# A hybrid decoder block: pacing copies on another engine, and level multiplications joined over two token halves

## The chip, the cores and the metric

The kernel runs on one core of a Trainium2 chip. TensorE (PE) multiplies matrices into PSUM, and its weight loads (PEld) overlap its multiplications. VectorE (DVE), ScalarE (ACT) and GpSimd (POOL) work on tiles in SBUF and PSUM, and SyncE (SP) issues most of the DMA transfers. Each engine runs its own list of instructions in the order in which it stands, and waits on semaphores for the other engines and for the DMAs. The metric is the time of one execution in microseconds (us).

## What is computed

One decoder layer on 256 tokens of width 1024, in float32. From one input projection two token mixers are fed, a gated linear recurrence (HGRN2) and an attention over blocks; both are projected, mixed through sigmoid gates, and followed by a layer norm, a SwiGLU network of width 2816 and a second layer norm. The parts that matter here:

```python
def hgrn2_mixer(q, f_logit, inp, lb):
    ...
    k = (1.0 - lb) * jax.nn.sigmoid(-z)
    qf = jax.nn.silu(q.astype(jnp.float32))
    ...
    def step(state, xs):
        qc, kc, vc, lfc = xs
        G = jnp.cumsum(lfc, axis=2)
        diff = G[:, :, :, None, :] - G[:, :, None, :, :]
        decay = jnp.exp(jnp.where(causal, diff, -jnp.inf))
        scores = jnp.einsum('bhtsd,bhtd,bhsd->bhts', decay, qc, kc)
        ...

def hybrid_layer(x, w_in, lb, ...):
    proj = jnp.einsum('bsd,dn->bsn', x, w_in)
    hq, hf, hi, hg, mq, mk, mv, gate_logits = jnp.split(proj, offsets, axis=-1)
    o_a = hgrn2_mixer(...)
    y_a = rms_norm(o_a, ...) * jax.nn.silu(hg)
    ...
    mixed = jnp.einsum('bsc,cd->bsd', g_a * z_a + g_b * z_b, w_out)
    x = layer_norm(DN_ALPHA * x + mixed, ln1_w, ln1_b)
    ...
    return layer_norm(DN_ALPHA * x + y, ln2_w, ln2_b)
```

## The kernel before

**The weight stream.** All weights are cut into 89 blocks of 1 MB (128 x 2048 floats), used in a fixed order. `stage` brings one in: SyncE loads it into one of three raw buffers (line 233), ScalarE casts it to a rounded high half `wh` (line 236), and VectorE subtracts that from the raw block for the low half `wl` (line 238). There are four buffers for each half. A product with such a weight is made of three matmuls, high by high, high by low and low by high. When the subtraction of a block ends, its raw buffer is free, and the load of the block three places on can be issued. Blocks are counted from 0 below.

**The weight sums.** Three of the big projections (hg, mv and the last one of the feed-forward network) are done in seven block products where eight would be usual (`quad_stage`, `quad_product`). They need sums of weight blocks, which GpSimd makes with 32 DMA transfers into DRAM, some of them copies and some with addition. `sum_weights` (line 247) issues one of them, paced by the weight stream. A tick, one element of a staged block, is copied into `ticks` (line 253); GpSimd adds it to itself into `mark` (line 254), and only then issues the transfer (line 256). `SUMS_WITH` names the block for each tick; most are blocks 2 to 16 and 56 to 67.

**The recurrence.** `hgrn_steps` (line 478) works out the scores in seven levels. On level l the tokens are taken in groups of n = 2^l. `KL` gathers the keys of the earlier groups (line 506, ScalarE), TensorE multiplies them with the queries of the later ones (line 514), VectorE writes the results into `SD` under a mask (line 516), and then the queries `Qt` and the keys `Kt` are multiplied by the groups' totals of the forget gate (lines 524 and 525, VectorE). The totals for the next level are products of pairs (line 528). The tokens are in two halves of 128, the second of them in reverse order, so the offsets in the two halves differ, and the multiplications of lines 524 and 525 run once for each half. Each step of the recurrence is woven between two stages of the weight stream.

**The stage of hg and ga.** Blocks 12 to 22 alternate between products for hg (`quad_stage`, line 607) and pairs of the gate ga (`gate_pair`, line 642). Block 17 is the fourth product of hg: lines 623 and 624 take it out of PSUM on VectorE. Block 18 is the fifth; line 627 stands behind block 18's product in the text, but needs only results up to block 17. Block 19 is for ga, block 20 for hg, block 21 for ga and block 22 for hg. The silu of hg (line 665, ScalarE) comes when a part of it is complete.

**What sets the order.** Outside of a few stretches that are written out by hand, a scheduler orders the instructions of each engine by its own estimate of times. So a change in one place can move instructions that it does not name.

Of the kernel before, what the change touches and what calls it, by code (L numbers as in the profile page):

```python
# [17 lines left out]
P = 128  # L18
T = 256
NT = T // P  # L20
D = 1024
KC = D // P
H = 8
# [121 lines left out]
def hybrid_layer_kernel(ctx: ExitStack, tc, x, xw, vecs, wts, ln1_w, ln1_b, ln2_w, ln2_b, consts, out):  # L145
    nc = tc.nc
# [16 lines left out]
    def r32(ap):  # L163
        return ap.bitcast(F32)
# [52 lines left out]
    def stage(pieces=None, eng=nc.vector):  # L217
        i = state["next"]
        if i >= len(loads):
            return  # L220
        state["next"] += 1
        at, k, held = loads[i]
        src = source(at).rearrange("p (k c) -> p k c", k=k)
        view = lambda z: z.rearrange("p (k c) -> p k c", k=k)
        home, tag = (late, "late") if state.get("four") and i % 4 == 0 else (wraw, "raw")
        raw = view(home.tile([P, 2048], F32, tag=tag, name=f"raw{i}"))
        if held:
            h, l = view(slot(f"wh{i}", F32R)), view(slot(f"wl{i}", F32R))
        else:
            h = view(whi.tile([P, 2048], F32R, tag="h", name=f"wh{i}"))  # L230
            l = view(wlo.tile([P, 2048], F32R, tag="l", name=f"wl{i}"))
        for ks in ks_of(pieces or (k,)):
            load = nc.sync.dma_start(raw[:, ks, :], src[:, ks, :])
            if i < EARLY:
                tc.keep_in_program_order(load)
            nc.scalar.copy(h[:, ks, :], raw[:, ks, :])  # L236
            yield
            eng.tensor_sub(l[:, ks, :], raw[:, ks, :], r32(h[:, ks, :]))  # L238
            yield
        ready.append((h, l))  # L240
        for _ in range(SUMS_WITH.count(i)):
            sum_weights(r32(l[:, 0, 0:1]))

    mark = cp.tile([P, 1], F32, tag="mark", name="mark")
    ticks = cp.tile([P, len(sums)], F32, tag="ticks", name="ticks")
# [1 line left out]
    def sum_weights(behind):  # L247


        n = len(SUMS_WITH) - len(sums)  # L250
        dst, src, add = sums.pop(0)
        tick = ticks[:, n:n + 1]
        nc.vector.tensor_copy(tick, behind)  # L253
        tc.keep_in_program_order(nc.gpsimd.tensor_tensor(mark, tick, tick, op=ALU.add))  # L254
        more = dict(accum_op=ALU.add, max_dma_last_dim=2048) if add else {}
        tc.keep_in_program_order(nc.gpsimd.dma_start(source(dst), source(src), **more))  # L256
# [151 lines left out]
    Fg, Kt, Qg = halves(slot("Fg")), halves(slot("Kt")), halves(slot("Qg"))  # L408
# [28 lines left out]
    for j in range(4):  # L437
# [6 lines left out]
        for f in range(2):  # L444
            h = 2 * j + f
# [12 lines left out]
    def free_view(ap, offset, dims):  # L458
        return bass.AP(ap.tensor, ap.offset + offset, [ap.ap[0]] + dims)
# [18 lines left out]
    def hgrn_steps():  # L478
# [17 lines left out]
        for l in range(LEVELS):  # L496
            n = 2 ** l
            nb = 64 // n
            KL = klp.tile([P, H, P], F32, tag="kl", name=f"kl{l}")
            if l == 0:  # L500
                pair = KL.rearrange("p h t -> p (h t)")
                nc.vector.tensor_mul(KL.rearrange("p h (u b i) -> p u h b i", u=NT, i=n), earlier(Kt, n), later(Qt, n))
                parts = slot("k0", F32R)[:, 0:D]
                fold(parts[:, 0:D], pair, kqt[:, 0:D])
            else:
                nc.scalar.copy(KL.rearrange("p h (b u i) -> p u h b i", u=NT, i=n), earlier(Kt, n))
            for g in range(2):
                ps = aux.tile([P, 4, P], F32, tag="aux", name=f"sc{l}_{g}")
                if l == 0:
                    row = ps.rearrange("p h t -> p (h t)")  # L510
                    nc.tensor.matmul(row, ones, parts[:, g * 512:(g + 1) * 512], start=True, stop=True)
                for a in range(4 if l else 0):
                    h = 4 * g + a
                    nc.tensor.matmul(ps[:, a, :], KL[:, h, :], later(Qt, n, h, 1), start=True, stop=True)  # L514
                m = masks[:, l, :].rearrange("p (u b i) -> p u b i", u=NT, i=n)
                nc.vector.copy_predicated(later(SD, n, 4 * g, 4),
                                          m[:, :, None, :, :].to_broadcast([P, NT, 4, nb, n]),
                                          ps.rearrange("p a (u b i) -> p u a b i", u=NT, i=n))

            side = lambda z, off, u: free_view(z, off + u * H * P, [[2 * n, H * nb], [1, n]])  # L520
            whole = lambda off: free_view(tot, off, [[2, H * nb], [0, n]])
            for u in range(NT):
                q, k = side(Qt, n - u * n, u), side(Kt, u * n, u)
                nc.vector.tensor_mul(q, q, whole(u * (size // NT + 1)))
                nc.vector.tensor_mul(k, k, whole(1 + u * (size // NT - 1)))
            if l < LEVELS - 1:
                nxt = Tt[:, off:off + size // 2]
                nc.vector.tensor_mul(nxt, free_view(tot, 0, [[2, size // 2]]), free_view(tot, 1, [[2, size // 2]]))
                off += size // 2
                tot, size = nxt, size // 2  # L530
            yield
# [534 lines left out]
```

## Time and profile before

| | us |
|---|---|
| median of the runs shown | 492.84 |
| lowest and highest of them | 492.49, 805.31 |
| span of the profiled execution | 491.3 |

The span goes from the first to the last instruction of one profiled execution; its own time is not among the runs shown, which stand about 1.5 us above the span (492.84 - 491.3). The run at 805.31 is far from the two others.

In the views, L236 is line 236 of the kernel. A row names engine, operation and tiles as output<-inputs, without buffer numbers. "Idle before" is the time in which the engine stood before the instruction, with what ended it. In a timeline the first number is the start from the beginning of the span and the second the duration.

### The profile page before, as it was taken

The numbers are of one execution on the slowest core, as the hardware profiler recorded it, in microseconds if no ns is written. First come the engines' busy times: TensorE is split into PE (matmuls) and PEld (weight loads), VectorE is DVE, ScalarE is ACT, GpSimd is POOL, SyncE is SP. The second block draws the span as 40 slices with busy tenths as digits, with TensorE's granted clock in tenths as the row PEclk, the third lists the DMA queues.
The fourth block names the chain that finished last, engine by engine and source line by source line (L and its number), as shares of the span: only waits on it lengthen the run. The fifth ranks groups of instructions, "written<-read, shape, count | busy, mean of one in ns | idle before, by whom it ended". The sixth has DMA issues, their size and how long they took to land.

```text
span 491.3 us, 7536 instructions
## 1 busy us (share of the span) xinstructions
PE 482.9 (98%) x2980; PEld 434.0 (88%) x2980; DVE 396.2 (81%) x490; ACT 315.6 (64%) x446; POOL 66.0 (13%) x89
## 2 busy tenths in 40 slices
PE   9999999999999999999999999999999999999994
PEld 9999888888888999999989988888888888898883
DVE  4888899999879869999773999555886779589947
ACT  6797677655879869789762555444565656587700
POOL 2305150530000010010010000001213010000001
PEclk9999999999999999999999999999999999999998
DMA  8879899999996988669776466049999999999702
GB/s 315 371 263 448 273 294 339 316 356 300 343 330 248 318 300 301 229 228 338 255 268 248 177 257 233 18 176 407 286 307 354 317 310 308 297 361 387 257 0 85
DMA packets 25106, 137.79 MB, mean 280 GB/s; under 512 B 2416, under 2 KB 2544, under 8 KB 13424
## 3 DMA queue, kind: packets, MB, share of 16 engines
q1 hardware_dynamic: 15264, 100.63, 53.2%
q0 software_dynamic: 9808, 36.70, 29.0%
q8 instruction: 23, 0.38, 0.3%
q14 instruction: 11, 0.09, 0.0%
HBM read 136.27 MB, written 34.60 MB: 348 GB/s over the span
## 4 chain that ended last, share of the span: by engine, by line
PE 95%; DVE 2%; DMA 2%; issue 0%; ACT 0%; DVEq 0%
PE fu L315 7%; PE fg L315 7%; PE fg L316 3%; PE fu L316 3%; PE gb L315 3%; PE za L315 3%; PE wd L999 2%; PE wd L1000 2%; PE wd L1001 2%; DMA raw<-in_wts_dram 2%; PE sc L514 2%; PE hf L383 2%; PE ga L315 2%; PE hf L384 2%; PE mk L355 2%; PE zb L355 2%
## 5 line engine op out<-in xcount | busy, mean ns | idle before, releaser
L238 DVE TENSOR_TENSOR wl<-raw,wh 128x2048 fp32r<-128x2048 f32 x89 | 203.0, 2289 | 54.0 <-ACT wh L236 53.5
L236 ACT CAST wh<-raw 128x2048 fp32r<-128x2048 f32 x89 | 169.8, 1916 | 73.9 <-PE fg L315 17.6
L315 PE MATMUL fg<-x1p,wh 128*128 128x512 f32 x144 | 50.5, 394 | 0.0
L315 PE MATMUL fu<-x1p,wh 128*128 128x512 f32 x144 | 50.4, 394 | 0.0
L254 POOL TENSOR_TENSOR mark<-ticks 128x1 f32<-128x1 f32 x32 | 24.4, 762 | 180.8 <-DVE ticks L253 159.9
L316 PE MATMUL fg<-x1p,wl 128*128 128x256 f32 x144 | 40.0, 277 | 0.0
L316 PE MATMUL fu<-x1p,wl 128*128 128x256 f32 x144 | 39.9, 277 | 0.0
L315 PEld LDWEIGHTS fu<-x1p,wh 128*128 128x128 f32 x144 | 27.0, 187 | 6.2
L315 PEld LDWEIGHTS fg<-x1p,wh 128*128 128x128 f32 x144 | 27.0, 187 | 6.1
L316 PEld LDWEIGHTS fg<-x1p,wl 128*128 128x128 f32 x144 | 27.0, 188 | 0.1
L316 PEld LDWEIGHTS fu<-x1p,wl 128*128 128x128 f32 x144 | 27.0, 188 | 0.0
L315 PE MATMUL za<-yP,wh 128*128 128x512 f32 x64 | 23.6, 407 | 0.0
L315 PE MATMUL gb<-xP,wh 128*128 128x512 f32 x64 | 22.7, 397 | 0.0
L315 PE MATMUL ga<-xP,wh 128*128 128x512 f32 x64 | 22.6, 396 | 0.0
L256 POOL DMA_DIRECT2D u<-in_wts_dram x24 | 19.7, 827 | 9.7 <-DMA u<-in_wts_dram 7.3
L353 PE MATMUL mq<-xP,wh 128*128 128x256 f32 x64 | 18.6, 291 | 0.0
L354 PE MATMUL mk<-xP,wh 128*128 128x256 f32 x64 | 18.4, 288 | 0.0
L353 PE MATMUL mk<-xP,wh 128*128 128x256 f32 x64 | 18.3, 285 | 0.0
L316 PE MATMUL za<-yP,wl 128*128 128x256 f32 x64 | 18.3, 285 | 0.0
L355 PE MATMUL mq<-xP,wl 128*128 128x256 f32 x64 | 18.2, 284 | 0.0
L355 PE MATMUL mk<-xP,wl 128*128 128x256 f32 x64 | 18.1, 283 | 0.0
L353 PE MATMUL hq<-xP,wh 128*128 128x256 f32 x64 | 18.1, 283 | 0.0
(338 smaller groups left out, 1388.3 us busy)
## 6 DMA issues: line engine op xcount, KB each, us to landing
raw<-in_wts_dram SPq DMA_DIRECT2D x73, 1024.0 KB, 6.3
raw<-u SPq DMA_DIRECT2D x16, 1024.0 KB, 6.7
u<-in_wts_dram POOLq DMA_DIRECT2D x8, 1024.0 KB, 20.5
u<-u POOLq DMA_DIRECT2D x8, 1024.0 KB, 18.2
first<-in_xw_dram SPq DMA_DIRECT2D x6, 640.0 KB, 9.3
xr<-in_x_dram POOLq DMA_DIRECT2D x1, 1024.0 KB, 5.2
wb<-in_ln_w_dram POOLq DMA_DIRECT2D x2, 512.0 KB, 6.6
wb<-in_ln_b_dram POOLq DMA_DIRECT2D x2, 512.0 KB, 7.9
```

The costliest lines, as they stand in the source:

```text
L236: nc.scalar.copy(h[:, ks, :], raw[:, ks, :])
L238: eng.tensor_sub(l[:, ks, :], raw[:, ks, :], r32(h[:, ks, :]))
L254: tc.keep_in_program_order(nc.gpsimd.tensor_tensor(mark, tick, tick, op=ALU.add))
L256: tc.keep_in_program_order(nc.gpsimd.dma_start(source(dst), source(src), **more))
L315: nc.tensor.matmul(ps, wh[:, k, wcol], a.both(k), start=(k == 0), stop=False)
L316: nc.tensor.matmul(ps[:, 0, :], wl[:, k, wcol], a[0, k, slice(0, T)], start=False, stop=(k == KC - 1))
L353: nc.tensor.matmul(ps, wh[:, k, wcol], ah[:, kk, :], start=(kk == 0), stop=False)
L354: nc.tensor.matmul(ps, wh[:, k, wcol], al[:, kk, :], start=False, stop=False)
L355: nc.tensor.matmul(ps, wl[:, k, wcol], ah[:, kk, :], start=False, stop=(kk == KC - 1))
L383: nc.tensor.matmul(pss[f], wh[:, wcol], xTh[:, k, :], start=(k == 0), stop=False)
L384: nc.tensor.matmul(pss[f], wh[:, wcol], xTl[:, k, :], start=False, stop=False)
L514: nc.tensor.matmul(ps[:, a, :], KL[:, h, :], later(Qt, n, h, 1), start=True, stop=True)
```

## The change

It has two edits. The tick is copied by ScalarE, and from the high half of the block, which ScalarE has cast, and no longer from the low half that VectorE has made. And each pair of level multiplications, one for each token half, becomes one instruction with a further dimension over the halves, whose step is the distance between their offsets. The values computed are the same.

```diff
         for _ in range(SUMS_WITH.count(i)):
-            sum_weights(r32(l[:, 0, 0:1]))
+            sum_weights(r32(h[:, 0, 0:1]))
...
-        nc.vector.tensor_copy(tick, behind)
+        nc.scalar.copy(tick, behind)
...
-            side = lambda z, off, u: free_view(z, off + u * H * P, [[2 * n, H * nb], [1, n]])
-            whole = lambda off: free_view(tot, off, [[2, H * nb], [0, n]])
-            for u in range(NT):
-                q, k = side(Qt, n - u * n, u), side(Kt, u * n, u)
-                nc.vector.tensor_mul(q, q, whole(u * (size // NT + 1)))
-                nc.vector.tensor_mul(k, k, whole(1 + u * (size // NT - 1)))
+            side = lambda z, off, gap: free_view(z, off, [[gap, NT], [2 * n, H * nb], [1, n]])
+            whole = lambda off, gap: free_view(tot, off, [[gap, NT], [2, H * nb], [0, n]])
+            q, k = side(Qt, n, H * P - n), side(Kt, 0, H * P + n)
+            nc.vector.tensor_mul(q, q, whole(0, size // NT + 1))
+            nc.vector.tensor_mul(k, k, whole(1, size // NT - 1))
```

The changed text is one line shorter, so what was line 623 is line 622 now. The scheduler orders the instructions anew. GpSimd and SyncE keep theirs; the other three differ in places, most of them between blocks 4 and 31.

VectorE before, from the subtraction of block 17 (`wl_1250`) to that of block 19 (`wl_1288`); `wl_1269` is block 18, and `hg_1155` is the product that block 17 feeds:

```order
L238 TENSOR_TENSOR wl_1250<-raw_1248,wh_1249 128x2048
L525 TENSOR_TENSOR Kt<-Kt,Tt 128x16x32 x2
L326 TENSOR_TENSOR ga<-ga_1292,ga 128x256
L238 TENSOR_TENSOR wl_1269<-raw_1267,wh_1268 128x2048
L326 TENSOR_TENSOR ga<-ga_1309,ga 128x256
L623 TENSOR_TENSOR hgs<-hgp,hg_1155 128x512
L624 TENSOR_TENSOR hgs<-hg_1155,hgs 128x512
L627 TENSOR_TENSOR hgs<-hgs 128x512
L238 TENSOR_TENSOR wl_1288<-raw_1286,wh_1287 128x2048
```

VectorE after, the same stretch; blocks 17, 18 and 19 are `wl_1240`, `wl_1259` and `wl_1278`, and the product of block 17 is `hg_1147`:

```order
L238 TENSOR_TENSOR wl_1240<-raw_1238,wh_1239 128x2048
L326 TENSOR_TENSOR ga<-ga_1282,ga 128x256
L326 TENSOR_TENSOR ga<-ga_1299,ga 128x256
L622 TENSOR_TENSOR hgs<-hgp,hg_1147 128x512
L623 TENSOR_TENSOR hgs<-hg_1147,hgs 128x512
L238 TENSOR_TENSOR wl_1259<-raw_1257,wh_1258 128x2048
L626 TENSOR_TENSOR hgs<-hgs 128x512
L238 TENSOR_TENSOR wl_1278<-raw_1276,wh_1277 128x2048
```

The subtraction of block 18 moved behind the second ga sum and behind both operations on the product of block 17. On TensorE block 18 follows block 17 directly, before as after.

ScalarE before, from the hg copy ahead of block 18 (`wh_1268`) to the silus behind block 19 (`wh_1287`):

```order
L620 COPY hgs<-hg_1154 128x512
L325 COPY ga<-ga_1292 128x256
L236 CAST wh_1268<-raw_1267 128x2048
L650 ACTIVATE ga<-ga,vec 128x256
L325 COPY ga<-ga_1309 128x256
L650 ACTIVATE ga<-ga,vec 128x256
L236 CAST wh_1287<-raw_1286 128x2048
L665 ACT_TABLE_LOAD
L665 ACTIVATE hgs<-hgs 128x512
L640 COPY hgs<-hg_1152 128x512
L665 ACTIVATE hgs<-hgs 128x512
```

ScalarE after, with block 17 (`wh_1239`), block 18 (`wh_1258`) and block 19 (`wh_1277`):

```order
L619 COPY hgs<-hg_1146 128x512
L236 CAST wh_1239<-raw_1238 128x2048
L325 COPY ga<-ga_1282 128x256
L649 ACTIVATE ga<-ga,vec 128x256
L325 COPY ga<-ga_1299 128x256
L236 CAST wh_1258<-raw_1257 128x2048
L649 ACTIVATE ga<-ga,vec 128x256
L664 ACT_TABLE_LOAD
L664 ACTIVATE hgs<-hgs 128x512
L236 CAST wh_1277<-raw_1276 128x2048
L639 COPY hgs<-hg_1144 128x512
L664 ACTIVATE hgs<-hgs 128x512
```

Three casts moved: that of block 17 behind the hg copy, that of block 18 behind the second ga copy, and that of block 19 behind the table load and the first silu.

TensorE before, at the end of block 20 (`wh_1333`, `wl_1334`) and the start of block 21 (`wh_1353`, `wl_1354`):

```order
L331 MATMUL hg_1155<-wh_1333,xSh 128x512
L332 MATMUL hg_1155<-wl_1334,xSh 128x512
L333 MATMUL hg_1155<-wh_1333,xSl 128x512
L315 MATMUL ga_1462<-xP_88,wh_1353 128x512
L315 MATMUL ga_1479<-xP_88,wh_1353 128x512
```

TensorE after, at the start of block 20 (`wh_1323`, `wl_1324`), with the first two matmuls of block 21 (`wh_1343`):

```order
L331 MATMUL hg_1147<-wh_1323,xSh 128x512
L315 MATMUL ga_1450<-xP_88,wh_1343 128x512
L315 MATMUL ga_1467<-xP_88,wh_1343 128x512
L332 MATMUL hg_1147<-wl_1324,xSh 128x512
L333 MATMUL hg_1147<-wh_1323,xSl 128x512
```

Before, all twelve matmuls of block 20 stood ahead of the first one of block 21, and all of block 21 ahead of the first one of block 22. Now block 21's first two come after one matmul of block 20; block 22's first one comes after the remaining eleven, ahead of the rest of block 21.

## The prediction

> **What bounds the kernel now.** I read the profile's page first: the busy shares and the chain that ended last.
>
> ```profile
> span 491.3 us, 7536 instructions
> PE 482.9 (98%) x2980; PEld 434.0 (88%) x2980; DVE 396.2 (81%) x490; ACT 315.6 (64%) x446; POOL 66.0 (13%) x89
> PE 95%; DVE 2%; DMA 2%; issue 0%; ACT 0%; DVEq 0%
> ```
>
> TensorE is busy for 482.9 of 491.3 us and 95% of the chain runs over it, so time can be won only where it stands still, and every new halt is paid in full. The second view is that of who waited for whom, for TensorE alone. It has two rows:
>
> ```profile
> PE warm L425 <- PEq L1053: 0.8, 1, 0.8
> PE mv L332 <- DVE wl L238: 0.2, 1, 0.2
> ```
>
> A busy row can hide a halt, since the ends of matmuls are modelled. So I read start-to-start times in TensorE's timeline at the two places where it is slowest in its stride:
>
> ```profile
> 136.85 0.39 PE L331 MATMUL hg<-wh,xSh 128*128 128x512 f32 x1
> 137.33 0.50 PE L332 MATMUL hg<-wl,xSh 128*128 128x512 f32 x1
> 137.67 0.40 PE L333 MATMUL hg<-wh,xSl 128*128 128x512 f32 x1
> 137.90 0.39 PE L331 MATMUL hg<-wh,xSh 128*128 128x512 f32 x1
> ...
> 150.03 0.39 PE L331 MATMUL mv<-wh,xP 128*128 128x512 f32 x1
> 150.59 0.50 PE L332 MATMUL mv<-wl,xP 128*128 128x512 f32 x1 [0.17 <-DVE wl L238]
> 150.93 0.40 PE L333 MATMUL mv<-wh,xP 128*128 128x512 f32 x1
> ```
>
> The normal stride of a 512-column matmul is 0.23 us (137.67 to 137.90). The strides 0.48, 0.34, 0.56 and 0.34 are over it by 0.25, 0.11, 0.33 and 0.11: 0.80 us in all, the low halves of blocks 20 and 23 coming late. That is what is to be won in the weight stream. The rest of the span without TensorE is the last layer norm, which the change does not touch.
>
> The third view is the busy time by stretches. VectorE is full (19.93 of 20) in the stretch in which most of the level multiplications stand:
>
> ```profile
> 95.00:115.00 20.00, 20.00 (x122) 17.68 (x121) 19.93 (x30) 10.08 (x15) 4.91 (x6) 1.00 1.04 347
> ```
>
> (Columns: the stretch, its length, then busy time and instructions of PE, PEld, DVE, ACT and POOL, the granted clock, the DMA share and GB/s.)
>
> **The change part by part.** First the work itself, from the groups by line:
>
> ```profile
> L238 DVE TENSOR_TENSOR wl<-raw,wh 128x2048 fp32r<-128x2048 f32 x89 | 203.0, 2289 | 54.0 <-ACT wh L236 53.5
> L525 DVE TENSOR_TENSOR Kt<-Kt,Tt 128x512 f32<-128x512 f32 x12 | 7.7, 687 | 0.0
> L253 DVE COPY ticks<-wl 128x1 f32<-128x1 f32 x32 | 4.6, 144 | 0.0
> L502 DVE TENSOR_TENSOR kl<-Kt,Qt 128x1024 f32<-128x1024 f32 x1 | 1.2, 1218 | 0.0
> L421 ACT ACTIVATE act<-act 128x1 f32<-128x1 f32 x1 | 0.2, 203 | 0.0
> L719 ACT COPY pT<-pt 128x128 f32<-128x128 f32 x8 | 2.1, 263 | 2.2 <-DVE pTp L211 2.2
> ```
>
> VectorE loses 32 ticks of 0.144 (4.6 us). Its 28 level multiplications of 0.687 (19.2 us) become 14 of twice the size; the nearest row is the 128x1024 product of L502 at 1.218, so 17.1 us. Together 6.7 us less on VectorE. ScalarE gains 32 ticks; the trace has no one-element copy there, and the nearest rows bound it at 0.20 (a one-element activation) and 0.26 (a 128-element copy); I take 0.20, as it has the size, 6.5 us in all (8.3 at most). Both engines are beside TensorE, so by themselves these cost and save nothing beyond the 0.80 us above. ScalarE's cover is its idle time, 36% of the span; VectorE's saving falls where it is full, and it frees raw buffers sooner there.
>
> A tick now follows the cast of a block and no longer its subtraction. So GpSimd may start a sum up to a subtraction, 2.3 us, sooner, or the idle that ScalarE's order puts ahead of the tick later. GpSimd and SyncE keep their own order of instructions. A sum that starts 2 us either way stays hidden: a block's low half is formed 3 us or more ahead in most of the stream, and only sums that a load waits for could matter. I cost it at nothing; if that cover fails it is one load late, of the size of the halts below.
>
> Adding the two: by VectorE's relief alone the sum would be -0.80. In the Trainium skill, the page Perfetto Trace Analysis (Optimizing Scalar/DVE Operations) says the same in general: on a saturated engine, grouping into larger operations and offloading from VectorE to ScalarE can improve throughput. The trace agrees that VectorE is full in that stretch. By that rule alone the kernel would take 492.0 us; it is a rival below.
>
> What speaks against it is the order, which the change also writes anew. It is the main term. In the order of before, block 18's subtraction stands ahead of the two operations on the product hg of block 17; now it stands behind them (the rows are in the part on the change). The trace of before shows these operations:
>
> ```profile
> 123.62 2.29 DVE L238 TENSOR_TENSOR wl<-raw,wh 128x2048 fp32r<-128x2048 f32 x1 [1.38 <-ACT wh L236]
> ...
> 126.99 0.69 DVE L623 TENSOR_TENSOR hgs<-hgp,hg 128x512 f32<-128x512 f32 x1 [0.74 <-PE hg L333]
> 127.59 0.68 DVE L624 TENSOR_TENSOR hgs<-hg,hgs 128x512 f32<-128x512 f32 x1
> 128.31 0.69 DVE L627 TENSOR_TENSOR hgs<-hgs 128x512 f32<-128x512 f32 x1
> 128.92 2.29 DVE L238 TENSOR_TENSOR wl<-raw,wh 128x2048 fp32r<-128x2048 f32 x1
> 131.12 1.58 DVE L516 COPY_PREDICATED SD<-cst,sc 128x512 f32<-128x512 uint32 x2
> ```
>
> and TensorE beside them:
>
> ```profile
> 126.56 0.39 PE L333 MATMUL hg<-wh,xSl 128*128 128x512 f32 x1
> ...
> 127.02 0.39 PE L332 MATMUL hg<-wl,xP 128*128 128x512 f32 x1
> ...
> 129.51 0.62 PE L315 MATMUL ga<-xP,wh 128*128 128x512 f32 x2
> ...
> 131.66 0.36 PE L316 MATMUL ga<-xP,wl 128*128 128x256 f32 x1
> ```
>
> L623 waits for TensorE's last matmul of block 17 (126.56) and starts at 126.99. TensorE wants block 18's low half in the second matmul after that one, at 127.02. With the new order, L623 and L624 come first, so the subtraction takes the place of the third operation, 128.31, and ends 2.29 later at 130.60. TensorE stands from 127.02 to 130.60: **3.6 us**. No earlier arrival of anything shortens this: the subtraction is queued behind an operation that waits for TensorE itself.
>
> Next, block 19. ScalarE now has one silu ahead of block 19's cast, and that silu needs the result of L627, which is queued behind the late subtraction. Rows of ScalarE before:
>
> ```profile
> 126.70 1.90 ACT L236 CAST wh<-raw 128x2048 fp32r<-128x2048 f32 x1
> 128.61 1.28 ACT L665 ACT_TABLE_LOAD   x1
> 129.91 0.63 ACT L665 ACTIVATE hgs<-hgs 128x512 f32<-128x512 f32 x1
> 130.44 0.57 ACT L640 COPY hgs<-hg 128x512 f32<-128x512 f32 x1
> ```
>
> L627 starts 2.20 after the subtraction (128.92 to 131.12), at 130.51, and ends at 131.20; the silu takes 0.63, the cast overlaps it by 0.10 and takes 1.90: 133.63. TensorE, by now 3.58 late, wants it at 129.51 + 3.58 = 133.09: 0.54 us, which makes it 4.12 late. The subtraction after the cast takes 2.29 and ends at about 135.94, and TensorE wants it at 131.66 + 4.12 = 135.78: 0.16 us. Together **0.7 us**, and TensorE is 4.3 late.
>
> Then the loads. There are three raw buffers, so the load of block n+3 is issued when block n's subtraction ends. Block 21's load leaves at 130.60 and no longer at 125.94, block 22's at 135.94 and no longer at 131.24. Their landing times by the DMA view, for the loads issued at 125.94, 131.24, 137.30 and 140.38, and the median of the whole run:
>
> ```profile
> raw<-in_wts_dram SPq DMA_DIRECT2D x1, 1024.0 KB, 10.2
> raw<-u SPq DMA_DIRECT2D x1, 1024.0 KB, 9.3
> raw<-in_wts_dram SPq DMA_DIRECT2D x1, 1024.0 KB, 9.0
> raw<-in_wts_dram SPq DMA_DIRECT2D x1, 1024.0 KB, 8.7
> ...
> raw<-in_wts_dram SPq DMA_DIRECT2D x73, 1024.0 KB, 6.3
> ```
>
> TensorE's new order asks for both blocks sooner: block 21 after one matmul of block 20, at 136.85 + 4.3 + 0.2 = 141.4, and block 22 two 512-column matmuls and eleven more (13 x 0.23 = 3.0) later, at 144.4. With 9.0 us of flight and 1.9 of cast, block 21 is there at 141.5 and block 22 at 146.8: 0.1 and 2.4 late, **2.5 us**. With 6.3 us nothing is late (0); with 10.2 and 9.3 it is 1.4 and 1.5, 2.9 us. I take 9.0, the flight at the very time.
>
> The old halts of 0.80 us fall inside the new ones, since the loads of blocks 23 and later now have more time than before. Sum: 3.6 + 0.7 + 2.5 - 0.8 = 6.0 us. Against the profiled span: 491.3 + 6.0 = 497.3. The median of the runs shown, 492.84, is 1.5 above that span (what lies around it), so **498.8 us**, 1.2% slower.
>
> A second rule is weighed here. The same page of the Trainium skill (Identifying the Most-Contended Engine) says that matmul busy time is no good measure of how near TensorE is to its limit, and that weight-load busy time should be used instead. By that, 434.0 us (88%) would leave room, and relief on VectorE could win several times 0.80 us. The strides of 0.23 us in the timeline do not show such room, so I give it next to no chance.
>
> **The rivals.**
> Relief only, faster: the halts at 137.33 and 150.59 vanish and nothing new comes: 492.84 - 0.80 = 492.0. For it speaks VectorE's full row; against it that L623 waits for TensorE and block 18's subtraction is queued behind it. It decides if the subtraction ends before TensorE asks for it, 3.6 us sooner than I work out. 0.10.
>
> The halt is there but the loads keep up (6.3 us of flight): 492.84 + 3.6 + 0.7 - 0.8 = 496.3. This is in my forecast's own range.
>
> Slower by over 2%: the blocks before 18 run dry too. ScalarE now casts block 17 behind the copy of hg (L620):
>
> ```profile
> 118.60 0.59 ACT L620 COPY hgs<-hg 128x512 f32<-128x512 f32 x1
> ...
> 124.28 0.40 PE L332 MATMUL hg<-wl,xSh 128*128 128x512 f32 x1
> ```
>
> That copy starts at 118.60, so the cast runs from 119.1 to 121.0 and the subtraction ends at 123.3, against TensorE's 124.28: 1.0 us of margin. If its load, now issued later, lands 3 us after the copy, 2 us are lost there and at block 16 alike, and with the upper end of the loads 3.6 + 0.7 + 2.9 + 4 = 11.2: 504 us. 0.08.
>
> No effect: the new order is absorbed and the old halts stay: 492.8. It asks for the same 3.6 us as relief. 0.06.
>
> **How the numbers follow.** Forecast with its loads slow or quick: 0.76; relief only 0.10; no effect 0.06; over 2% slower 0.08. The time is that of the likeliest case, 498.8. The range runs from 495.0 (the halt alone, 492.84 + 3.6 + 0.7 - 0.8 = 496.3, less 1.3 for a shorter chain at block 18) to 502.0 (no old halt won back and the loads at their upper end, 492.84 + 3.6 + 0.7 + 2.9 = 500.0, and 2 us at blocks 16 and 17); it leaves out about 0.2. A difference of 2%, about 9.9 us here, is what a measurement of this kernel can tell from no change. By that the chances are 0.01 faster (the whole gain is 0.8 us), 0.91 the same, 0.08 slower.
>
> **What would show it.** In the profile after, TensorE's waits should have a row of hg L332 for wl of about 3.5 us, near 127 us of the span; VectorE's subtraction for block 18 should start right behind L623 (its old L624); a wait of under 1 us at ga behind it; and one or two waits for casts of blocks 21 and 22, 0 to 3 us. VectorE's busy time should fall by 6 to 7 us and ScalarE's rise by 6 to 8. If TensorE has no row for wl there, the main term is wrong; if the row is there and the time is not longer, the halt was won back later, which a full TensorE does not allow.

## The result, and the profile after

| | before | changed |
|---|---|---|
| median of the comparison, us | 493.06 (6 runs) | 498.13 (6 runs) |
| lowest and highest, us | 492.49, 805.31 | 497.76, 604.13 |
| ratio of the times, 95% interval | | 1.0109 [1.0093, 1.0125] |
| span of the profiled execution, us | 491.3 | 495.9 |

The change makes the kernel 1.1% slower: the interval lies clear of 1, and the difference is under 2%. The runs at 604.13 and 805.31 us are disturbed executions and are left out of the ratio. The rows of the changed kernel below are those of its run e1_changed (498.04 us for the profiled execution, so 2.1 us lie around its span).

First the page of the changed kernel: its span, the busy time of each engine, and the chain that ended last.

```profile
span 495.9 us, 7509 instructions
PE 483.3 (97%) x2980; PEld 434.0 (88%) x2980; DVE 392.7 (79%) x444; ACT 319.1 (64%) x478; POOL 80.2 (16%) x89
PE 95%; DMA 2%; DVE 1%; ACT 1%; issue 1%; DVEq 0%
```

TensorE has the same work as before (483.3 against 482.9 us busy) in a span that is 4.6 us longer. So TensorE stands still longer. The view of TensorE's waits names the places (columns: who waited, for what, us in total, times, longest):

```profile
PE hg L332 <- DVE wl L238: 3.4, 1, 3.4
PE hg L331 <- ACT wh L236: 0.9, 1, 0.9
PE warm L425 <- PEq L1052: 0.8, 1, 0.8
PE ga L315 <- ACT wh L236: 0.3, 1, 0.3
```

The row of `warm` was there before. The three others are new, and their total, 4.6, is as much as the span grew. TensorE's timeline of the changed kernel shows the three places, from the start-to-start times:

```profile
126.75 0.39 PE L331 MATMUL hg<-wh,xP 128*128 128x512 f32 x1
130.49 0.50 PE L332 MATMUL hg<-wl,xP 128*128 128x512 f32 x1 [3.35 <-DVE wl L238]
130.83 0.40 PE L333 MATMUL hg<-wh,xP 128*128 128x512 f32 x1
...
132.89 0.39 PE L333 MATMUL hg<-wh,xP 128*128 128x512 f32 x1
133.55 0.74 PE L315 MATMUL ga<-xP,wh 128*128 128x512 f32 x2 [0.28 <-ACT wh L236]
...
144.16 0.39 PE L333 MATMUL hg<-wh,xSl 128*128 128x512 f32 x1
145.41 0.50 PE L331 MATMUL hg<-wh,xP 128*128 128x512 f32 x1 [0.86 <-ACT wh L236]
```

Less the normal stride of 0.23 us, the halts are 3.51 at block 18 (126.75 to 130.49), 0.11 and 0.43 behind it (130.49 to 130.83, 132.89 to 133.55), and 1.02 at block 22 (144.16 to 145.41).

VectorE's timeline of the changed kernel at the first place shows what TensorE waited for:

```profile
126.95 0.69 DVE L622 TENSOR_TENSOR hgs<-hgp,hg 128x512 f32<-128x512 f32 x1 [1.95 <-PE hg L333]
127.55 0.68 DVE L623 TENSOR_TENSOR hgs<-hg,hgs 128x512 f32<-128x512 f32 x1
128.16 2.28 DVE L238 TENSOR_TENSOR wl<-raw,wh 128x2048 fp32r<-128x2048 f32 x1
130.35 0.68 DVE L626 TENSOR_TENSOR hgs<-hgs 128x512 f32<-128x512 f32 x1
133.53 2.29 DVE L238 TENSOR_TENSOR wl<-raw,wh 128x2048 fp32r<-128x2048 f32 x1 [2.50 <-ACT wh L236]
```

VectorE was idle for 1.95 us ahead of L622, because L622 waits for TensorE's last matmul of block 17. Block 18's subtraction was queued behind it and ended at 130.44, and TensorE went on at 130.49.

The halt at block 19 has another cause. ScalarE's timeline shows its cast behind a silu, which waits for L626, the operation behind the late subtraction:

```profile
131.07 0.63 ACT L664 ACTIVATE hgs<-hgs 128x512 f32<-128x512 f32 x1 [3.02 <-DVE hgs L626]
131.61 1.89 ACT L236 CAST wh<-raw 128x2048 fp32r<-128x2048 f32 x1
```

The halt at block 22 hangs on its load. These are SyncE's issues of the loads of blocks 21 and 22 in the changed kernel:

```profile
130.46 0.33 SPq L233 DMA_DIRECT2D raw<-in_wts_dram  x1
135.85 0.33 SPq L233 DMA_DIRECT2D raw<-u  x1
```

and the DMA view of the same two moments, whose last number is the time from issue to landing:

```profile
raw<-in_wts_dram SPq DMA_DIRECT2D x1, 1024.0 KB, 8.0
raw<-u SPq DMA_DIRECT2D x1, 1024.0 KB, 7.6
```

They leave right behind the late subtractions of blocks 18 and 19 (128.16 + 2.28 and 133.53 + 2.29). Block 22 lands at 135.85 + 7.6 = 143.45, its cast takes 1.91, and TensorE gets it at 145.41, 1.02 us late. Block 21 lands in time.

The groups by line of the changed kernel show the work that was moved:

```profile
L523 DVE TENSOR_TENSOR Qt<-Qt,Tt 128x1024 f32<-128x1024 f32 x6 | 7.3, 1222 | 0.0
L253 ACT COPY ticks<-wh 128x1 f32<-128x1 f32 x32 | 6.2, 195 | 0.2
```

So far this is the halt that was foreseen. What the profile cannot tell is which of the two edits wrote the new order, whether a fix of the order alone would win the time back, and whether the copies cost something by themselves.

### The profile page after: what moved, and what is told of

It is laid out like the page before. It is cut to its first block, busy times and chain, and to the rows that moved or that the text cites. A ratio compares the mean times of both kernels' runs of the same rounds, so it can differ in the third digit from the quotient of the medians.

```text
span 602.0 us, 7509 instructions
## 1 busy us (share of the span) xinstructions
PE 590.6 (98%) x2980; PEld 495.1 (82%) x2980; DVE 396.3 (66%) x444; ACT 321.2 (53%) x478; POOL 78.9 (13%) x89
## 4 chain that ended last, share of the span: by engine, by line
PE 98%; DVE 1%; issue 0%; DVEq 0%
PE fg L315 7%; PE fu L315 7%; PE fu L316 3%; PE fg L316 3%; PE ga L315 3%; PE za L315 3%; PE gb L315 3%; PE wd L1000 2%; PE wd L998 2%; PE sc L514 2%; PE wd L999 2%; PE gb L316 2%; PE mk L354 2%; PE zb L355 2%; PE mq L354 2%; PE zb L353 2%
## 5 line engine op out<-in xcount | busy, mean ns | idle before, releaser
L238 DVE TENSOR_TENSOR wl<-raw,wh 128x2048 fp32r<-128x2048 f32 x89 | 203.3, 2290 | 101.6 <-ACT wh L236 101.2
L254 POOL TENSOR_TENSOR mark<-ticks 128x1 f32<-128x1 f32 x32 | 36.9, 1154 | 243.6 <-ACT ticks L253 243.6
L315 PE MATMUL fu<-x1p,wh 128*128 128x512 f32 x144 | 61.7, 456 | 0.0
L315 PE MATMUL fg<-x1p,wh 128*128 128x512 f32 x144 | 61.6, 459 | 0.0
L316 PE MATMUL fg<-x1p,wl 128*128 128x256 f32 x144 | 45.7, 318 | 0.0
L316 PE MATMUL fu<-x1p,wl 128*128 128x256 f32 x144 | 45.2, 314 | 0.0
L315 PE MATMUL za<-yP,wh 128*128 128x512 f32 x64 | 28.5, 475 | 0.0
L315 PE MATMUL gb<-xP,wh 128*128 128x512 f32 x64 | 27.6, 454 | 0.0
L315 PE MATMUL ga<-xP,wh 128*128 128x512 f32 x64 | 27.5, 464 | 0.0
L353 PE MATMUL mq<-xP,wh 128*128 128x256 f32 x64 | 20.5, 320 | 0.0
L316 PE MATMUL gb<-xP,wl 128*128 128x256 f32 x64 | 20.4, 318 | 0.0
L354 PE MATMUL mq<-xP,wh 128*128 128x256 f32 x64 | 20.2, 316 | 0.0
```

Source lines behind the costliest of these rows:

```text
L315: nc.tensor.matmul(ps, wh[:, k, wcol], a.both(k), start=(k == 0), stop=False)
L316: nc.tensor.matmul(ps[:, 0, :], wl[:, k, wcol], a[0, k, slice(0, T)], start=False, stop=(k == KC - 1))
L353: nc.tensor.matmul(ps, wh[:, k, wcol], ah[:, kk, :], start=(kk == 0), stop=False)
L354: nc.tensor.matmul(ps, wh[:, k, wcol], al[:, kk, :], start=False, stop=False)
```

## The experiments

Each run was compared with runs of the kernel before on the same chip. All of them compute the whole layer. Where a run "holds" an order, each instruction of TensorE, VectorE and ScalarE is tied, without any wait, to the one that stands ahead of it in another kernel's order of that engine:

```diff
+    for order in ORDERS.values():
+        order = [n for n in order if f"I-{n}" in traced]
+        for a, b in zip(order, order[1:]):
+            tc.add_manual_dep(traced[f"I-{b}"], f"I-{a}", mybir.DependencyInfo(
+                mybir.DependencyClass.NoSync, mybir.DependencyReason.DATA), reason="order")
```

The diffs are against the changed kernel, but for e8's; `...` stands for lines left out, and the lines that hold an order are not repeated.

**e1_changed.** The changed kernel as it is, for a profile.

> The changed kernel once more, for a profile at the full clock. Theory (order): TensorE waits about 3.5 us for the low half of block 18 at L332, near 127 us of the span, under 1 us at block 19, and 0 to 3 us for the casts of blocks 21 and 22; 497.5 to 498.7 us. Rival (ScalarE's load: the 32 ticks make ScalarE late everywhere): no single wait over 1 us, the loss is spread over many blocks.

498.14 against 492.84 us, 1.0106 [1.0080, 1.0132]. Its rows are those above.

**e2_block18_first.** In the changed kernel, the two operations on block 17's product are kept behind block 18's subtraction.

```diff
-            eng.tensor_sub(l[:, ks, :], raw[:, ks, :], r32(h[:, ks, :]))
+            lows[i] = eng.tensor_sub(l[:, ks, :], raw[:, ks, :], r32(h[:, ks, :])).ins
...
-        nc.vector.tensor_sub(dst[:, 1, lo], p, b[3])
-        nc.vector.tensor_sub(dst[:, 1, hi], b[3], dst[:, 1, hi])
+        with tc.issue_after(lows[18]) if name == "hg" else ExitStack():
+            nc.vector.tensor_sub(dst[:, 1, lo], p, b[3])
+            nc.vector.tensor_sub(dst[:, 1, hi], b[3], dst[:, 1, hi])
```

> The changed kernel with one pin: the two operations on the product of block 17 (L622, L623) are issued behind block 18's subtraction. On VectorE that one row moves, on ScalarE the casts of blocks 19 and 20 move ahead of a silu; all else is as in the changed kernel, ticks on ScalarE and joined multiplications with it. Theory (order): the 3.6 us halt shrinks to what block 18's late cast leaves (cast to 126.4, subtraction to 128.7, wanted at 127.0: 1.7 us), and the 0.7 us at block 19 goes; 493.5 to 495.5 us. Rival (ScalarE's load): 498 us, nothing of the load has changed.

496.62 us, 1.0082 [1.0051, 1.0112]: a miss. TensorE's waits in it, where each line number is one higher than in the changed kernel:

```profile
PE hg L332 <- ACT wh L237: 1.7, 1, 1.7
PE hg L333 <- DVE wl L239: 1.6, 1, 1.6
PE sd L490 <- DVE kqh L477: 1.5, 1, 1.5
```

The halt at block 18 fell from 3.4 to 1.6, as far as was expected of it. But the cast of block 22 now costs 1.7, and a third halt, at `sd` for `kqh`, is 50 us earlier in the program, where this edit changes nothing. So something besides the order at block 18 is late. This profiled execution took 498.28 us and the three others 496.51 to 496.63, so the halt at `sd` is probably not in those.

**e3_block18_both.** As e2, and ScalarE's second ga copy is kept behind block 18's cast.

```diff
-            nc.scalar.copy(h[:, ks, :], raw[:, ks, :])
+            highs[i] = nc.scalar.copy(h[:, ks, :], raw[:, ks, :]).ins
...
-            nc.scalar.copy(dst[f], z[:, 1, :])
+            with tc.issue_after(highs[18]) if behind and f else ExitStack():
+                nc.scalar.copy(dst[f], z[:, 1, :])
...
```

> As the run before, and on ScalarE the cast of block 18 is also pinned ahead of the copy of the second ga sum. Theory (order): no halt over 0.5 us at block 18, and the old halts at blocks 20 and 23 are gone or small; 491.8 to 493.5 us. Rival (ScalarE's load): 498 us.

496.52 us, 1.0074 [1.0051, 1.0097]: a miss too. TensorE waited 1.8 us for block 21's cast, 1.2 for block 18's low half and 0.4 for block 22's cast. There is no halt at `sd`. What halts TensorE is the rest of the new order, which this run keeps: ScalarE's cast of block 18 still stands behind an operation of the gate that waits for VectorE (123.21, the cast at 123.62), and TensorE still asks for block 21 after one matmul of block 20. By strides, less the normal 0.23, these halts are 1.35 at block 18 (126.32 to 127.90), 1.91 at block 21 (137.91 to 140.05) and 0.57 at block 22 (142.91 to 143.71).

**e4_joined_only.** Only the joined multiplications; the copies stay on VectorE.

```diff
-            sum_weights(r32(h[:, 0, 0:1]))
+            sum_weights(r32(l[:, 0, 0:1]))
...
-        nc.scalar.copy(tick, behind)
+        nc.vector.tensor_copy(tick, behind)
```

> The level multiplications joined, the ticks left on VectorE. Its order keeps block 18's subtraction ahead of the operations on block 17's product. Theory (order): no halt at block 18; 491.8 to 493.5 us, the 14 instructions of 128x1024 take 1.2 us each. Rival (the joined multiplications hold VectorE too long in one piece): 495 us or more, with waits behind L523 and L524.

493.05 us, 1.0007 [0.9993, 1.0021]: no difference. The joined multiplications neither cost nor bring anything, and the scheduler leaves block 18 where it was.

**e7_ticks_only.** Only the copies on ScalarE, reading the high half; the multiplications stay in pairs.

```diff
...
-            q, k = side(Qt, n, H * P - n), side(Kt, 0, H * P + n)
-            nc.vector.tensor_mul(q, q, whole(0, size // NT + 1))
-            nc.vector.tensor_mul(k, k, whole(1, size // NT - 1))
+            for u in range(NT):
+                q, k = side(Qt, n - u * n, u), side(Kt, u * n, u)
+                nc.vector.tensor_mul(q, q, whole(u * (size // NT + 1)))
+                nc.vector.tensor_mul(k, k, whole(1 + u * (size // NT - 1)))
```

> The ticks on ScalarE, the multiplications in halves, the order as the scheduler gives it: block 18's subtraction stands behind the first operation on block 17's product, ahead of the second. Theory (order): a halt of 3.0 us at block 18 (0.6 less than 3.6), less at blocks 19 to 22, 495 to 498.5 us. Rival (joined multiplications are at fault): 492.5 to 493.5 us.

497.08 us, 1.0083 [1.0068, 1.0098]. Block 18's subtraction stands behind the first operation on block 17's product and ahead of the second, and TensorE's two large waits are like those of the changed kernel:

```profile
PE hg L332 <- DVE wl L238: 2.6, 1, 2.6
PE hg L331 <- ACT wh L236: 1.3, 1, 1.3
```

Thus the edit of the copies alone makes block 18 late and brings most of the loss.

**e6_old_work_new_order.** The work and the diff of e4 (copies on VectorE, from the low half), with the three engines held to the changed kernel's order.

> The other corner: the ticks stay on VectorE, each right behind its subtraction, the multiplications are joined, and the three engines are held to the order of the changed kernel. Theory (order): as slow as the changed kernel or a little slower, 497.5 to 500 us, with the 3.5 us wait of L332 for block 18. Rival (ScalarE's load): 492.5 to 493.5 us, as ScalarE has no tick.

497.71 against 493.24 us, 1.0097 [1.0083, 1.0111]. TensorE has one new halt, `PE hg L332 <- DVE wl L238` of 3.4 us. The order alone is enough for the main term, whichever engine makes the copies. The total is not the order's alone, though: in this profile TensorE's granted clock was 0.50 from 131.5 to 134.9 us, behind the halt, and the strides were 0.42 us in place of 0.23. In the profile of the changed kernel the clock stayed at 1.00 there.

**e8_block18_late_before.** The kernel before, with only the subtractions of blocks 18 to 20 put behind the operations on block 17's product, and line 627 behind the first of them.

```diff
-            eng.tensor_sub(l[:, ks, :], raw[:, ks, :], r32(h[:, ks, :]))
+            if i in (18, 19, 20):
+                held_back.append((l, raw, h))
...
+        for n, (l, raw, h) in enumerate(held_back):
+            with tc.issue_after(last.ins):
+                last = nc.vector.tensor_sub(l, raw, r32(h))
...
```

(The diff is against the kernel before.)

> The kernel before, with the subtractions of blocks 18 to 20 pinned behind the two operations on block 17's product; ticks on VectorE and multiplications in halves, casts and loads up to there as before. Theory (order): L332 waits 3.5 us at block 18, and the loads of blocks 21 and 22 leave 4 us later; 495.5 to 499 us. Rival (ScalarE's load, or the loads alone): 492.8 to 494 us.

497.44 us, 1.0092 [1.0071, 1.0112]: the total as expected, the place not. TensorE waited only 0.5 us for block 18's low half, and 2.9 us at ga for casts, nearly all of it for block 21's. In this kernel the scheduler put block 19's first two products and 16 score products between block 18's first and second matmul, which covered the wait. Block 18's subtraction still ended at 130.18 (127.90 + 2.28 in VectorE's timeline) where it had ended at 125.9, and block 21's load, which waits for that buffer, left as much later. The time was lost all the same, a few us further on. Part of the total is again the clock, 0.50 from 142.2 to 145.7 us behind the halt for block 21: the two executions with a mean granted clock of 0.994, the profiled one among them, took 498.01 and 498.86 us, the two with 0.997 and 0.996 took 496.48 and 496.87.

**e5_change_old_order.** Both edits as in the changed kernel, with the three engines held to the order of e4, and each copy on ScalarE right behind its cast.

> Both edits, but VectorE, ScalarE and TensorE are held to the order of the run with joined multiplications alone, each tick right behind the cast of its block. Theory (order): the work itself costs nothing, 491.8 to 493.5 us, and no wait over 0.7 us of TensorE on the weight stream. Rival (ScalarE's load by the ticks): 496 us or more, since the 32 ticks stand on ScalarE as in the changed kernel.

496.39 against 493.24 us, 1.0069 [1.0056, 1.0081]: a miss, and the one that mattered. With the order of before, 3 us are still lost. TensorE's waits in it have one large row, and no row for a weight block:

```profile
PE sd L489 <- DVE kqh L476: 3.0, 1, 3.0
```

It is the halt that e2 had shown. `sd` is the product that reads `kqh`, and VectorE makes `kqh` behind the subtractions of blocks 8 and 9. VectorE's timeline in e4, without the halt:

```profile
65.37 4.48 DVE L238 TENSOR_TENSOR wl<-raw,wh 128x2048 fp32r<-128x2048 f32 x2
69.78 0.14 DVE L253 COPY ticks<-wl 128x1 f32<-128x1 f32 x1
69.94 2.28 DVE L476 TENSOR_TENSOR kqh<-Qg,kqh 64x2048 fp32r<-64x2048 f32 x1
```

and in e5:

```profile
69.40 4.48 DVE L238 TENSOR_TENSOR wl<-raw,wh 128x2048 fp32r<-128x2048 f32 x2
73.91 2.29 DVE L476 TENSOR_TENSOR kqh<-Qg,kqh 64x2048 fp32r<-64x2048 f32 x1
```

The same instructions in the same order run 4 us later. ScalarE's casts show where VectorE fell behind. The cast of block 6 in e4:

```profile
45.51 1.91 ACT L236 CAST wh<-raw 128x2048 fp32r<-128x2048 f32 x1 [1.51 <-PE hq L354]
```

and in e5:

```profile
51.20 1.91 ACT L236 CAST wh<-raw 128x2048 fp32r<-128x2048 f32 x1 [6.82 <-DMA raw<-in_wts_dram]
```

Block 6 came 5.7 us later, for want of its load. That load was issued at the same time in both, but two sums had been sent off before it in e5 and none in e4. Two theories were then open: the sums that start sooner hold up the load (A), or ScalarE's copies are what costs (B). (The expectations below count that block as block 5; it is block 6, counted from 0.)

The halt cost more than its length, since the clock fell behind it. The busy time by stretches (columns as in the prediction's third view, so the clock is the third number from the end), first in e4 and then in e5:

```profile
75.00:90.00 15.00, 15.00 (x92) 13.26 (x92) 14.94 (x19) 11.00 (x13) 0.00 (x0) 1.00 1.00 320
75.00:90.00 15.00, 13.75 (x68) 11.73 (x69) 14.91 (x14) 12.63 (x18) 5.64 (x6) 0.89 0.97 287
```

In e5 the granted clock was 0.50 from 75.8 to 79.2 us, and from `sd` to the third matmul of gb with a high half TensorE took 3.09 us (76.25 to 79.34) in place of 1.59 (72.98 to 74.57). So the halt of 3.0 cost some 1.5 us more behind it.

**e9_sums_early_vector, e10_sums_late_scalar, e11_first_eight_late.** All three have the joined multiplications and the order of e4. In e9 VectorE makes the copies, from the high half, as soon as the cast is done. In e10 ScalarE makes them, from the low half, when VectorE did in e4. In e11 ScalarE makes them, the first eight as in e10 and the rest as in e5.

```diff
 e9:
-        nc.scalar.copy(tick, behind)
+        nc.vector.tensor_copy(tick, behind)
 e10:
-            sum_weights(r32(h[:, 0, 0:1]))
+            sum_weights(r32(l[:, 0, 0:1]))
 e11:
-            sum_weights(r32(h[:, 0, 0:1]))
+            sum_weights(r32((l if i < 10 else h)[:, 0, 0:1]))
```

> The joined multiplications with the 32 pacing copies on VectorE, but each reads the high half (as in the changed kernel) and stands on VectorE at the place where that cast had ended in the run of the joined multiplications alone, ahead of the subtraction; TensorE, ScalarE and the rest of VectorE are held to that run's order. So the weight sums start as early as in the run of both edits in the old order (first one sent off near 35 us instead of 38 us), with no copy on ScalarE. Theory A (the 3 us of that run come from the sums: sent off 3 to 5 us sooner, their transfers share the DMA engines with the loads of blocks 5 to 9, the cast of block 5 comes at 51 us instead of 45.5 us, the subtractions slide, and the last subtraction of kqh at 73 us, which stands behind them on VectorE, comes 3 to 4 us late): 495.5 to 497.5 us, with one halt of 2 to 4 us at the product sd behind kqh near 73 us. Theory B (the 3 us come from ScalarE's 32 copies): 492.5 to 493.8 us, no halt over 1 us.

499.53 against 493.00 us, 1.0116 [1.0076, 1.0156], a larger loss than theory A gave, with no copy on ScalarE. TensorE's wait in it:

```profile
PE sd L489 <- DVE kqh L476: 4.8, 1, 4.8
```

Block 6 was cast at 53.25, 2.0 us later than in e5, and behind the halt the clock was 0.50 from 78.7 to 82.1 us, which cost 1.7 us as reckoned for e5 (from `sd` to the fifth matmul of gb with a high half 3.98 in place of 2.30).

> Both edits of the change in the old order again, but the pacing copies on ScalarE read the low half, as VectorE's did, and stand on ScalarE at the next instruction after the time at which VectorE's copy ran in the run of the joined multiplications alone: the sums start no sooner than before the change, and ScalarE still makes all 32 copies. Theory A (early sums collide with the loads): 492.5 to 493.8 us, no halt over 1 us, block 5 cast near 45.5 us. Theory B (the copies on ScalarE cost it): 495.5 to 497.5 us, with a halt of 2 to 4 us at sd near 73 us or at another product that waits for ScalarE.

494.10 us, 1.0027 [1.0012, 1.0042], no halt over 0.8 us. This is 0.3 above theory A's range, and 1.4 below theory B's. The 1.1 us over the kernel before were not followed up.

> As the run of both edits in the old order, with all copies on ScalarE, but only the copies of blocks 2 to 9 read the low half and stand late as in the run before this one; the 24 others stay right behind their casts, early. Theory A in its narrow form (only the first eight sums collide, in the stretch of 35 to 75 us where the DMA engines are full): 492.5 to 494.0 us, no halt over 1 us near 73 us. Theory A in its wide form (the later early sums delay the loads of blocks 11 to 23 as well): 494.5 to 497 us, with halts of 1 to 3 us behind casts or subtractions of weight blocks between 80 and 160 us. Theory B: 495.5 to 497.5 us with the halt at sd near 73 us.

493.57 us, 1.0011 [0.9997, 1.0025], no halt over 0.5 us besides `warm`: theory A in its narrow form. In the old order only the first eight sums matter; the 24 others may start early.

Theory B falls. With the moments at which SyncE issued the load of block 6 and GpSimd sent off the first two sums, and the load's time to landing, the profiles line up (us):

| kernel | load issued | first sum | second sum | load's time to landing |
|---|---|---|---|---|
| e11 | 37.54 | 41.80 | 43.05 | 5.7 |
| e10 | 37.13 | 41.39 | 43.05 | 5.4 |
| before | 37.30 | 38.53 | 39.38 | 5.8 |
| e4 | 36.87 | 38.10 | 38.95 | 5.8 |
| e12 (below) | 37.34 | 37.91 | 41.69 | 8.6 |
| e6 | 37.01 | 36.98 | 38.37 | 10.7 |
| e5 | 36.88 | 34.65 | 36.85 | 14.2 |
| changed (e1) | 37.35 | 35.11 | 37.32 | 14.2 |
| e9 | 38.04 | 35.71 | 37.98 | 14.8 |

A sum that is sent off 1.2 us behind the load costs it nothing. One sent off with the load nearly doubles its time, and two ahead of it take it from 5.8 to over 14 us.

**e12_changed_low_half.** The changed kernel with one word put back: ScalarE's copy reads the low half. The scheduler orders everything.

```diff
-            sum_weights(r32(h[:, 0, 0:1]))
+            sum_weights(r32(l[:, 0, 0:1]))
```

> The changed kernel with one word put back: the pacing copy on ScalarE reads the low half of its block again, not the high half; nothing is held by hand, the scheduler orders everything. It then leaves block 18's subtraction ahead of the three operations on the gate, as before the change, and the sums start behind the subtractions. Theory A (both costs of the change, the halt at block 18 and the late loads, come from the copy's operand, which lets it start at the cast and which the scheduler's estimate follows; ScalarE's 6.5 us of copies and the joined multiplications cost nothing by themselves): 492.8 to 494.5 us, no halt over 1 us at hg, ga or sd. Theory B (some of the 5 us comes from the copies' being on ScalarE or from the joined multiplications, whatever the operand): 495 us or more.

492.68 against 493.51 us, 0.9986 [0.9970, 1.0002] (0.1 us under theory A's range): no difference from before, and the whole loss of the change is gone. TensorE's waits in it:

```profile
PE warm L425 <- PEq L1052: 0.8, 1, 0.8
PE mk L355 <- DVE wl L238: 0.3, 1, 0.3
```

VectorE's timeline in it shows block 18's subtraction in its old place, ahead of L622:

```profile
123.56 2.29 DVE L238 TENSOR_TENSOR wl<-raw,wh 128x2048 fp32r<-128x2048 f32 x1 [1.38 <-ACT wh L236]
125.77 0.42 DVE L326 TENSOR_TENSOR ga<-ga,ga 128x256 f32<-128x256 f32 x1
126.93 0.69 DVE L622 TENSOR_TENSOR hgs<-hgp,hg 128x512 f32<-128x512 f32 x1 [0.74 <-PE hg L333]
```

This answers what the profile could not: the loss comes neither from ScalarE's making the copies nor from the joined multiplications, but from the operand that the copy reads. It sets when the sums may start, and with it the order that the scheduler writes. How the scheduler's estimate gets from the one to the other was not looked into, and a copy by VectorE from the high half was run only in a held order (e9).

## Why the prediction was right, and where its steps were off

**The halt at block 18 (3.6 us) was right.** It measured 3.51 us, by the mechanism named: subtraction behind L623, L622 waiting for TensorE's block 17. e6 shows that the order alone makes this halt. e8 shows that block 18's late subtraction costs about as much even where other matmuls cover the first wait, though part of e8's total is the clock.

**Block 19 (0.7 us)** came at 0.43 for its cast (0.54 foreseen) and nothing for its low half (0.16). The mechanism was right: the cast behind the silu that waits for the late operation.

**The loads of blocks 21 and 22 (2.5 us) measured 1.02.** TensorE asked for block 22 at 144.16 + 0.23 = 144.39, where 144.4 was worked out, and the load was issued at 135.85, where 135.94 was. What was mis-sized is the flight: 9.0 us was taken, from the loads of the same stretch before, and it was 7.6. The 1.4 between them is the whole error of 2.4 against 1.02; of block 21's 0.1 nothing was left. The range given there (0 to 2.9) holds it. The rows point to a reason for the quicker flight, which no run tested apart: the last sum of this stretch left sooner. It was sent off at 120.53 and landed 22.5 us later, at 143.0, where before it was sent off at 124.59 and landed 25.4 later, at 150.0, so block 22's load had less of it beside it. In e2 and e3, where that sum landed at 148.0 and 146.7, the same load flew 9.3 and 9.5.

**The old halts (-0.8 us)** did vanish; none of them is among TensorE's waits after.

The sum of these is 3.51 + 0.54 (0.11 + 0.43) + 1.02 - 0.80 = 4.3, and the span grew by 4.6, where 6.0 was foreseen. The predicted time came out nearer than its terms, since the profiled execution has 2.1 us around its span and 1.5 were added: 1.4 too much in the terms and 0.6 too little around them. That two errors met was luck. The 1.5 set the median of several executions against the span of another one; where both are on record for one execution, the kernel before has 1.7 to 1.8 around its span and the changed kernel 2.1.

**"I cost it at nothing", on the sums that start sooner, was the step that failed without showing in the total.** The cover named for it, low halves formed well ahead, was not there near 40 us: block 6's load lands 14.2 us after its issue and no longer 5.8. The text gave the price if the cover fails, "one load late, of the size of the halts below", and e5 shows that price: a halt of 3.0 us, and the slow clock behind it. In the changed kernel it stays hidden, with little to spare. There VectorE has `kqh` ahead of block 9's subtraction:

```profile
68.09 2.28 DVE L238 TENSOR_TENSOR wl<-raw,wh 128x2048 fp32r<-128x2048 f32 x1
70.40 2.29 DVE L476 TENSOR_TENSOR kqh<-Qg,kqh 64x2048 fp32r<-64x2048 f32 x1
```

It ends at 72.69, and TensorE starts `sd` at 73.56: 0.9 us of margin. In e2's profiled execution, with the same operations in the same order there and block 6's cast at 53.49 in place of 51.60, that margin was gone and 1.5 us were lost. So the early sums cost 3.15 us in the old order (496.39 against 493.24, e5) and, as `sd` does not wait in the profile of the changed kernel, little or nothing in the new one, in which VectorE makes `kqh` one subtraction sooner. That is why so much was left when the whole old order was held.

It is not why e2 and e3 won only 1.5 and 1.6 of the 5.3 us back. e3 has no halt at `sd`, and its halts of 1.35, 1.91 and 0.57 us come from the parts of the new order that it kept.

**The busy times** moved half as far as foreseen. VectorE fell by 3.5 us (396.2 to 392.7) and not by 6 to 7, ScalarE rose by 3.5 (315.6 to 319.1) and not by 6 to 8, although the durations taken were right: a joined multiplication took 1.22 (1.218 foreseen), a copy on ScalarE 0.195 (0.20). What was wrong was to add up the durations of rows, which overlap at their edges. In e4's rows above, the subtractions run to 65.37 + 4.48 = 69.85, while the copy behind them starts at 69.78. In e7, where nothing but the copies left VectorE, it was busy for 394.0 us, 2.2 less: 0.07 us for each copy, half of its row of 0.144. The Trainium skill, on the page Perfetto Trace Analysis (Optimizing Scalar/DVE Operations), says of the overhead that each instruction has on these two engines that its profiled latency is about twice its engine-busy time, since the half that acknowledges the write overlaps with the next instruction; for VectorE's one-element copies the trace agrees (0.07 of 0.144). It changes nothing of the time here.

**The rivals.** Relief only (492.0) fell: e4 and e12 have the relief on VectorE without the halt, and they are at 1.0007 and 0.9986, so even the 0.8 us that was to be won is hardly seen. The rule that weight-load time tells TensorE's limit, from the same page of the Trainium skill (Identifying the Most-Contended Engine), which names it beside a second measure that was not weighed here, does not agree with this trace: that time is 434.0 us before and after, and 4.6 us of new halts made the span 4.6 us longer, so there was no room. Slower by over 2% did not come: block 17's subtraction ended at 123.27 and TensorE asked for it at 124.21, and neither block 16 nor block 17 has a row among the waits.

## What to carry to other kernels

When an instruction that only signals is moved to another engine, look at what it reads: its operand fixes the earliest moment of everything paced by it, and the scheduler's order may follow. Here the change of engine cost nothing and the change of operand cost 1%. When a bulk transfer may start sooner, find the loads that are issued within a few us of it and price them at up to two and a half times their flight (14.2 against 5.8 us here), even if the transfer itself is not waited for. And if removing one late instruction wins less than it cost, hold the whole old order before you pin the next one: what is left then is a cause that the new order hid, and the rest is the order's.

## What the runs showed of the hardware

**Sums and loads.** The loads and the sums do not share the DMA engines by bytes. The DMA view of the kernel before, 45 to 51 us, with sums and loads in flight (columns: packets, MB, share of the 16 engines' time; the sums are the software queue):

```profile
q0 software_dynamic: 53, 2.10, 85.4%
q1 hardware_dynamic: 57, 0.47, 18.8%
```

and that of the changed kernel, 39 to 45 us:

```profile
q0 software_dynamic: 49, 2.10, 81.9%
q1 hardware_dynamic: 75, 0.48, 19.5%
```

By the sizes of the single packets in the traces, 32 packets of 64 KB make up the 2.10 MB of the sums in both, and the loads have 57 and 59 packets of 8 KB; the rest are of 4 bytes. A packet of 64 KB took its engine for 2.5 us on the mean, one of 8 KB for 0.32. So the loads sent more packets of data than the sums and got less than a fifth of the bytes. The Trainium skill, on the page DMA: Bandwidth & Descriptors (Queues, rings and completion order), says that each DMA engine takes the queues that have work in turn and moves a whole packet from one before it goes on to the next; these counts are nearer to that than to equal bytes, but they are not equal, and no run shows that what the profile counts as a packet is what the page means. At 0.48 MB in 6 us a load of 1 MB would need some 13 us (an estimate from these rows); 14.2 were measured with two sums sent off ahead of it, and 5.8 with both sent off behind it.

It was not tried whether sums in smaller packets would leave the loads alone. The trace of the kernel before has a hint that they would not quite: from 134 to 138 us the sum in flight has packets of 2 KB alone (137 of them, beside 113 of 8 KB of loads), and the loads issued at 137.30 and 140.38 landed in 9.0 and 8.7 us, against a median of 6.3 in the whole run.

**The clock behind a halt.** In four of the profiles TensorE's granted clock fell to 0.50 for 3.4 us, beginning within 1.5 us of TensorE's going on after a halt: in e5 (halt of 3.0 us, clock low from 75.8), e6 (3.4, from 131.5), e8 (2.6, from 142.2) and e9 (4.8, from 78.7). In the profiles of the changed kernel (3.4), e7 (2.6) and e2 (1.5 to 1.7) it did not. What decides it is not shown. In e5 and e9 it cost 1.5 and 1.7 us beyond what the view of waits says.
